# Three edits to a two-block transformer kernel: where Down's operand lies, a mixer with blocks of 8, and products without a result

## The chip, the cores and the metric

The kernel runs on one core of one Trainium2 chip. The metric is the device time of one execution in microseconds; three runs were timed. One more execution was recorded by the hardware profiler, and every row below comes from that one. TensorE is called PE, VectorE DVE, ScalarE ACT, GpSimd POOL. A product is one matrix instruction of PE.

## The reference

256 rows of width 1024 pass through two layers of a first model and one layer of a second. In short:

```python
for i in range(2):
    x = x + 0.5 * swiglu(rms_norm(x, g[0]), gate, up, down)      # D_FF = 2816
    x = x + (even_mixer if i == 0 else mla_mixer)(rms_norm(x, g[1]))
    x = x + 0.5 * swiglu(rms_norm(x, g[2]), gate, up, down)
    x = x + per_layer_embedding(rms_norm(x, g[3]), p[i], ...)    # rms_norm(sigmoid(h Wg) * (p Wp))
x = x + hybrid_mixer(rms_norm(x, ...))
x = x + swiglu(rms_norm(x, ...), gate_up, down)
return rms_norm(x, norm_final)
```

So there are five feed-forward blocks. The even mixer, the "first mixer", splits `h @ w_in` into six parts; four of them (q, f, i, g) go to a gated linear recurrence with 4 heads of 128 and chunks of 64:

```python
b = cumsum(log f)                                    # inside a chunk of 64
scores[t, s] = sum_d q[t, d] * k[s, d] * exp(b[t, d] - b[s, d])    for s <= t
o = scores @ v + (q * exp(b)) @ state                # state carries over the chunks
o = rms_norm(o, out_norm) * silu(g)                  # norm over each head's 128
mixed = concat([a_out, o]) @ w_out
```

## The kernel before, in words

**Layout.** The residual stream `x` lies feature-major: eight tiles of 128 features by 256 rows. Each normalized operand is split in two float32r tiles, `hh` (high part) and `hl` (the rest); each weight likewise in `whi` and `wlo`. One product of the reference is three on PE: hh·whi, hl·whi, hh·wlo, each over 128 x 128 weights and 256 columns. Weights come in pieces of 2,048 columns by DMA on SP's queue; ACT copies each half to `whi` (L259) and DVE subtracts for `wlo` (L260). Six buffers of each exist, so the copy of half n+6 waits until PE has used half n.

**Places.** Tiles are laid out in a partition in the order in which they are first asked for, pool by pool. `hh` and `hl` (16 tiles of 1,024 bytes) begin at byte 99,776 and all lie at 448 modulo 512. The work tiles `big` (13 buffers of 4,096 bytes) begin at byte 153,664 and lie at 64 modulo 512. A feed-forward block first runs gate and up (1,056 products, moving operand `hh` or `hl`), then Down (528 products: 8 outputs, 22 inner blocks, 3 each), whose moving operand is the split activation `aT`, kept in `big` tiles. PE passes from the last product of gate and up to the first of Down without anything between. Weights lie at 128 modulo 512 throughout. A tile `pad` of 48 columns, which nothing uses, lies between `gu` and `nz`; what comes after it moves with its size: `nz`, `sqa`, `ny`, `rb`, `sg`, `pr`, `big` among them.

**Statistics.** `Stat.begin` multiplies the squares by a column of ones (moving operand `ones`, weights `sqa` or `sq`), DVE makes `ny`, the inverse root, and `Stat.finish` spreads it over the partitions with two transposes (`ident`, `ny`). In a feed-forward block these two groups stand among the first 160 products of gate and up; behind the second of them about 910 products run to the end of gate and up with no other group between.

**First mixer.** The scores inside a chunk of 64 are summed from a base (blocks of 4, one reference point for each block) and four levels (4, 8, 16, 32). Each level costs DVE two subtractions, two multiplications of 128x512 and two `COPY_PREDICATED` (L669), ACT one Exp, and PE eight full float32 products of 128 columns, which the trace records as sixteen. Then come the gates `g`, feature-major (`fm`, 96 products), the spatial part (`gm`), the attention output `og`, 16 ones-records for its norm, the first 72 products of the output projection, 8 broadcasts of the inverse root, DVE's multiplication (L821), the split (L273, L274), and the other 120 products.

**Order.** A scheduler writes each engine's instructions in one fixed order; an engine runs them in that order and waits at a semaphore where an operand isn't there yet.

Of the kernel before, what the change touches and what calls it, by code (L numbers as in the profile page):

```python
# [10 lines left out]
FT = mybir.dt.float32  # L11
FR = mybir.dt.float32r
# [5 lines left out]
P = 128  # L18
# [41 lines left out]
class Stat:  # L60
# [8 lines left out]
    def begin(self, ins=None, quick=False):  # L69
        k, nc = self.k, self.k.nc  # L70
        ps = k.aux()
        with k.behind(ins):
            last = len(self.parts) - 1
            for n, t in enumerate(self.parts):
                for b in range(NB):
                    k.mm(ps[:, b : b + 1], t[:, b * P : (b + 1) * P], k.ones, n == b == 0, n == last)
        v = k.tiny(NB, "nv")
        with k.tc.high_priority():
            y = None
            if quick:  # L80
                y = k.tiny(NB, "ny", bufs=6)
                self.mark = nc.scalar.activation(y, ps[:, :NB], AF.Sqrt, scale=1.0 / self.n, bias=k.eps).ins
            nc.vector.tensor_scalar(v, ps[:, :NB], 1.0 / self.n, EPS, op0=OP.mult, op1=OP.add)
            if quick:
                nc.vector.reciprocal(y, y)
        self.r = k.rsqrt(v, NB, y)

    def finish(self, ins=None, copy=True):
        k = self.k
        self.pb = pb = k.aux()[:, :T]  # L90
        with k.behind(ins):
            for b in range(NB):
                k.bcast(pb[:, b * P : (b + 1) * P], self.r[:, b : b + 1].to_broadcast([P, P]))
        return self.copy() if copy else self

    def copy(self):
# [10 lines left out]
class Kern:  # L107
# [54 lines left out]
    def mm(self, out, l, r, start=True, stop=True):  # L162
        return self.nc.tensor.matmul(out, l, r, start=start, stop=stop, skip_group_check=True).ins  # L163

    def behind(self, ins):
        return self.tc.issue_after(ins) if ins is not None else nullcontext()


    def constants(self):
# [40 lines left out]
            for c in range(D)  # L210
        ]

        self.sp.tile([P, 48], FT, name="pad", bufs=1)
        self.eps = cp.tile([P, 1], FT, name="eps")
        nc.vector.memset(self.eps, EPS)
        nc.scalar.activation(self.tiny(1, "nz"), self.ones, AF.Silu)
# [82 lines left out]

    def bcast(self, out, col, w=P):  # L300

        self.nc.tensor.transpose(out, col, self.ident)  # L302


    def sq_add(self, src, j, own=False):
# [196 lines left out]
    def ple(self, i, proj, rstd, post, gain, fill=None):  # L502
# [14 lines left out]

        self.fm([(("ple_w_gate", i), (d * P, P)) for d in range(D)], self.hT, evac, [2, 2, 2, 1, 1], k_first=True, stat=rstd)
        self.late = (self.piece + 2, 1), self.mark
        post_r = self.sq_end().now()  # L520
        more = fill() if fill else None


# [54 lines left out]
    def even(self, rstd, prep):  # L578
# [75 lines left out]
        def scores(kx, qx, lvl):  # L654
            for b in range(NB):
                ps = self.aux()
                for h in range(H):
                    o = slice(h * T + b * P, h * T + (b + 1) * P)
                    self.mm(ps[:, h * P : (h + 1) * P], kx[:, o], qx[:, o])
                p3 = ps.rearrange("p (h t) -> p h t", h=H)  # L660
                if lvl > 3:

                    l = 32 * (lvl - 3)
# [9 lines left out]


        d = self.big()
        b4 = bb.rearrange("p (m l) -> p m l", l=4)
        nc.vector.tensor_tensor(
            d.rearrange("p (m l) -> p m l", l=4), b4, b4[:, :, 1:2].to_broadcast([P, 256, 4]), op=OP.subtract
        )
        eq, ek = self.big(), self.big()  # L680
        nc.scalar.activation(eq, d, AF.Exp)
# [13 lines left out]
            nc.vector.tensor_tensor(xh[:, :, 1, :], xh[:, :, 1, :], qh[:, :, 1, :], op=OP.mult)  # L695
            scores(x, x, n + 1)

        level(0, 4)
        vi = self.cut([512, 512])

        def evac_i(b, ps):
# [1 line left out]

        self.tm(src, (2048, 512), self.hT, evac_i)

        for n, l in ((1, 8), (2, 16), (3, 32)):
            level(n, l)


# [8 lines left out]
        scores(x, x, 5)  # L718


        y = self.big()
# [19 lines left out]
        nc.scalar.activation(scA4[:, :, P:], ps.rearrange("p (h t) -> p h t", h=H), AF.Copy)  # L741


        sg = self.big()

        def evac_g(c, ps):
            o = slice(c * T, (c + 2) * T)
            self.scaled(sg[:, o], ps, rstd.rb)
            nc.scalar.activation(sg[:, o], sg[:, o], AF.Silu)

        self.fm([(src, (2560 + h * P, P)) for h in range(4)], self.hT, evac_g)

        gm = []
# [28 lines left out]
                gm.append((c, hi, lo))  # L784


        og = self.big()
        hs = self.aux()
        sqs = []
        for j in range(2):  # L790
            ps = self.aux()
            for u in range(2):
                h = 2 * j + u
                o = slice(u * T, (u + 1) * T)
                self.mm(ps[:, o], vi[0][:, h * P : (h + 1) * P], scA[:, h * T : (h + 1) * T], True, False)
                self.mm(
                    ps[:, u * T + P : (u + 1) * T], vi[1][:, h * P : (h + 1) * P],
                    scB[:, h * P : (h + 1) * P], False, True,
                )
# [4 lines left out]
            o = slice(j * 512, (j + 1) * 512)  # L804
            nc.vector.tensor_tensor(og[:, o], ps, sg[:, o], op=OP.mult)
# [5 lines left out]
        hv = self.tiny(8, "nv")  # L811
        nc.vector.tensor_scalar(hv, hs[:, :8], 1.0 / P, EPS, op0=OP.mult, op1=OP.add)
        hr = self.rsqrt(hv, 8)
        ks = []
        for j in range(2):
# [4 lines left out]
            o = slice(j * 512, (j + 1) * 512)  # L820
            nc.vector.tensor_tensor(og[:, o], og[:, o], ps, op=OP.mult)  # L821
            g2 = self.big(FR)
            hi, lo = g2[:, :512], g2[:, 512:]
            self.split(hi, lo, og[:, o], self.col("hgrn_out"))
            for u in range(2):
                ks.append((4 + 2 * j + u, hi[:, u * T : (u + 1) * T], lo[:, u * T : (u + 1) * T]))
# [590 lines left out]
    def load_small(self):  # L1417
        nc, a, cp = self.nc, self.a, self.cp

        def const(name, cols, dt=FT, eng=None):  # L1420
            t = cp.tile([P, cols], dt, name="k_" + name)
            (eng or nc.gpsimd).dma_start(t, a[name])
            return t

        self.tri = const("tri", P)
        self.amask = const("amask", 384)
        self.lvl = const("lvl", 4 * P, I32)
# [108 lines left out]
def constants():  # L1536
# [115 lines left out]
```

## Time and profile before

| what | value |
|---|---|
| median of 3 runs | 1332.64 us (1331.53 to 1332.75) |
| the profiled execution's own time | 1331.74 us |
| its span | 1330.0 us |
| PE busy | 1305.2 us (98%) |
| DVE, ACT, POOL busy | 922.9, 726.4, 76.1 us |
| mean granted clock of PE | 0.995 |

The span is what the profiler saw, the execution's own time has the start and end around it, 1.74 us. The profiled execution was 0.90 us faster than the median. PE is busy nearly all the time, so the table of busy shares alone says little: what counts is how fast PE's products follow each other in each stage, and the few places where it stands.

### The profile page before, as it was taken

How to read it: one execution, taken by the hardware profiler on the slowest of the kernel's cores; microseconds unless marked ns; L12 is line 12 of the kernel's file. 1: busy time of each engine (PE TensorE's matmuls, PEld its weight loads, DVE VectorE, ACT ScalarE, POOL GpSimd, SP SyncE). 2: the span in 40 equal slices, each digit the busy share in tenths (PEclk: the TensorE clock that was granted, in tenths of full speed). 3: DMA queues.
4: the chain of work that ended last, by engine and by line, in shares of the span. 5: the costliest groups of instructions: out<-in, count | busy, mean ns of one | idle time of the engine just before them, and what ended most of it. 6: DMA issues, size and time to landing. Idle time of an engine off the chain costs nothing.

```text
span 1330.0 us, 25894 instructions
## 1 busy us (share of the span) xinstructions
PE 1305.2 (98%) x10830; PEld 1275.3 (96%) x10830; DVE 922.9 (69%) x1528; ACT 726.4 (55%) x1110; POOL 76.1 (6%) x94
## 2 busy tenths in 40 slices
PE   9999999999999999999999899999998999999997
PEld 8999999899999999999999679999998998999997
DVE  7866657978666657966556867777557897867643
ACT  6555546646555456655545566554445685655542
POOL 3000010002000001000000002000002000200001
PEclk9999999999999999999999999999999999999999
DMA  8755555245555554465546313655555344455541
GB/s 320 262 190 187 174 196 181 95 162 188 190 190 188 185 210 159 163 219 190 190 162 220 127 64 116 205 191 196 185 186 183 135 142 143 164 207 198 194 159 64
DMA packets 34933, 235.50 MB, mean 177 GB/s; under 512 B 4016, under 2 KB 4784, under 8 KB 7168
## 3 DMA queue, kind: packets, MB, share of 16 engines
q1 hardware_dynamic: 32976, 229.98, 50.0%
q0 software_dynamic: 832, 2.47, 0.6%
q8 instruction: 85, 1.39, 0.4%
q10 hardware_dynamic: 1008, 1.40, 0.3%
q14 instruction: 32, 0.26, 0.1%
HBM read 232.78 MB, written 1.05 MB: 176 GB/s over the span
## 4 chain that ended last, share of the span: by engine, by line
PE 74%; DVE 5%; ACT 2%; issue 1%; DVEq 0%; ACTq 0%
PE acc L163 69%; PE aux L163 4%; DVE wlo L260 1%; PE aux L302 0%; ACT whi L259 0%; PE aux L1130 0%; DVE big L1175 0%; DVE qs L961 0%; ACT hh L273 0%; ACT at L1132 0%; DVE kv L961 0%; ACT ae L1122 0%; ACT big L949 0%; DVE big L514 0%; DVE big L429 0%
## 5 line engine op out<-in xcount | busy, mean ns | idle before, releaser
L260 DVE TENSOR_TENSOR wlo<-wraw,whi 128x1024 fp32r<-128x1024 f32 (+1 forms) x440 | 531.7, 1222 | 253.1 <-ACT whi L259 164.2
L259 ACT ACTIVATE whi<-wraw 128x1024 fp32r<-128x1024 f32 (+1 forms) x440 | 451.3, 1047 | 308.4 <-PE acc L163 221.4
L163 PE MATMUL acc<-hh,whi 128*128 128x256 f32 x2192 | 328.3, 279 | 3.4 <-ACT hh L538 3.1
L163 PE MATMUL acc<-hl,whi 128*128 128x256 f32 x2192 | 327.3, 278 | 0.2 <-DVE hl L543 0.2
L163 PE MATMUL acc<-hh,wlo 128*128 128x256 f32 x2192 | 326.3, 278 | 1.1 <-DVE wlo L260 1.1
L163 PEld LDWEIGHTS acc<-hh,whi 128*128 128x128 f32 x2192 | 286.0, 188 | 5.4 <-ACT hh L538 3.8
L163 PEld LDWEIGHTS acc<-hh,wlo 128*128 128x128 f32 x2192 | 286.0, 188 | 1.6 <-DVE wlo L260 1.4
L163 PEld LDWEIGHTS acc<-hl,whi 128*128 128x128 f32 x2192 | 286.1, 188 | 0.4 <-DVE hl L543 0.4
L163 PE MATMUL acc<-big,whi 128*128 128x256 f32 x2032 | 271.7, 280 | 0.0
L163 PEld LDWEIGHTS acc<-big,whi 128*128 128x128 f32 x2032 | 256.4, 189 | 0.4 <-ACT big L270 0.2
L163 PE MATMUL acc<-big,wlo 128*128 128x256 f32 x1016 | 161.7, 280 | 0.0
L163 PEld LDWEIGHTS acc<-big,wlo 128*128 128x128 f32 x1016 | 137.6, 189 | 0.0
L318 POOL TENSOR_TENSOR sqa<-sqa,sq 128x256 f32<-128x256 f32 x72 | 65.0, 903 | 1119.2 <-ACT sq L317 1117.1
L429 DVE TENSOR_TENSOR gu<-acc,rb 128x512 f32<-128x512 f32 (+1 forms) x122 | 81.9, 678 | 50.4 <-PE acc L163 50.1
L273 ACT ACTIVATE hh<-x,cols 128x256 fp32r<-128x256 f32 x64 | 30.3, 503 | 82.7 <-DVE x L468 79.2
L270 ACT ACTIVATE big<-pr 128x256 fp32r<-128x256 f32 x114 | 45.9, 409 | 52.0 <-DVE pr L447 50.2
L445 ACT ACTIVATE sg<-gu 128x256 f32<-128x256 f32 x110 | 44.8, 411 | 38.7 <-DVE gu L429 38.5
L271 DVE TENSOR_TENSOR big<-pr,big 128x256 fp32r<-128x256 f32 x114 | 47.8, 426 | 21.0 <-ACT big L270 21.0
L447 DVE TENSOR_TENSOR pr<-sg,gu 128x256 f32<-128x256 f32 x110 | 45.4, 419 | 2.2 <-ACT sg L445 2.2
L274 DVE SCALAR_TENSOR_TENSOR hl<-x,cols,hh 128x256 fp32r<-128x256 f32 x64 | 38.0, 619 | 8.6 <-ACT hh L273 8.3
L163 PE MATMUL aux<-big 128*128 128x128 f32 (+5 forms) x260 | 37.6, 310 | 0.8 <-DVE big L683 0.8
L317 ACT ACTIVATE sq<-x 128x256 f32<-128x256 f32 x62 | 23.9, 405 | 24.3 <-DVE x L470 18.2
(297 smaller groups left out, 788.5 us busy)
## 6 DMA issues: line engine op xcount, KB each, us to landing
wraw<-wts SPq DMA_DIRECT2D x216, 1024.0 KB, 4.9
wraw<-wts SPq DMA_DIRECT2D x4, 256.0 KB, 4.9
wraw<-wts SPq DMA_DIRECT2D x2, 512.0 KB, 5.4
x<-xT SPq DMA_DIRECT2D x2, 256.0 KB, 5.2
big<-wsT POOLq DMA_DIRECT2D x1, 512.0 KB, 13.3
gu<-pT ACTq DMA_DIRECT2D x2, 256.0 KB, 3.1
out<-big SPq DMA_DIRECT2D x2, 256.0 KB, 2.3
out<-big ACTq DMA_DIRECT2D x2, 256.0 KB, 2.5
```

Source lines behind the costliest of these rows:

```text
L163: return self.nc.tensor.matmul(out, l, r, start=start, stop=stop, skip_group_check=True).ins
L259: nc.scalar.activation(hi[:, i], s, AF.Copy)
L260: nc.vector.tensor_tensor(lo[:, i], s, hi[:, i].bitcast(FT), op=OP.subtract)
L270: a = nc.scalar.activation(hi, src, AF.Copy)
L271: b = nc.vector.tensor_tensor(lo, src, hi.bitcast(FT), op=OP.subtract)
L273: a = nc.scalar.activation(hi, src, AF.Copy, scale=scale)
L274: b = nc.vector.scalar_tensor_tensor(lo, src, scale, hi.bitcast(FT), op0=OP.mult, op1=OP.subtract)
L317: nc.scalar.activation(q, src, AF.Square)
L318: self.mark = nc.gpsimd.tensor_tensor(self.sq[0], self.sq[0], q, op=OP.add).ins
L429: self.nc.vector.tensor_tensor(out.rearrange("p (u t) -> p u t", u=n), ps.rearrange("p (u t) -> p u t", u=n), rb.unsqueeze(1).to_broadcast ...
L445: self.mark = nc.scalar.activation(sg, gu[:, :T], AF.Silu).ins
L447: nc.vector.tensor_tensor(pr, sg, gu[:, T:], op=OP.mult)
```

## The change

Three things. The tile `pad` shrinks from 48 to 16 columns and the constant `lvl` by 512 bytes, so `big` begins at byte 153,024, at 448 modulo 512, as `hh` and `hl` do; every other tile behind `pad` moves by the same 128 bytes modulo 512. The first mixer's base takes blocks of 8 and loses a level; its gates are made token-major (`tm`, 48 products of 512 columns), and so is the output with its norm: a reduction on DVE in place of the ones, a multiplication, and 8 transposes in place of the broadcasts. Behind the second embedding's last product, 8, 5 and 5 full float32 products of `ident` and `tri` into a bank that nobody reads are placed ahead of the sum, ahead of the spreading and after it.

```diff
+    def keep_on(self, ins, n):
+        ps = self.aux()
+        with self.tc.high_priority(), self.behind(ins):
+            for _ in range(n):
+                m = self.mm(ps[:, :P], self.ident, self.tri)
+        return m
...
-        self.sp.tile([P, 48], FT, name="pad", bufs=1)
+        self.sp.tile([P, 16], FT, name="pad", bufs=1)
...
-        post_r = self.sq_end().now()
+        post_r = self.sq_end()
+        if fill:
+            post_r.now()
+        else:
+            post_r.begin(self.keep_on(self.last, 8), quick=True)
+            post_r.finish(self.keep_on(post_r.summed, 5), copy=False)
+            self.keep_on(post_r.spread, 5)
...
-        b4 = bb.rearrange("p (m l) -> p m l", l=4)
+        b8 = bb.rearrange("p (m l) -> p m l", l=8)
...
-        level(0, 4)
...
-        for n, l in ((1, 8), (2, 16), (3, 32)):
+        for n, l in ((0, 8), (1, 16), (2, 32)):
             level(n, l)
...
-        self.fm([(src, (2560 + h * P, P)) for h in range(4)], self.hT, evac_g)
+        sg = self.cut([512, 512])
+        def evac_g(b, ps):
+            nc.scalar.activation(sg[b], ps, AF.Silu, scale=rstd.r[:, b : b + 1])
+        self.tm(src, (2560, 512), self.hT, evac_g)
...
+        for b in range(NB):
             ps = self.aux()
+            for h in range(H):
+                o = slice(h * P, (h + 1) * P)
+                self.mm(ps[:, o], scA4[:, h, b * P : (b + 1) * P], vi[0][:, o], h == 0, b == 0)
+                if b:
+                    self.mm(ps[:, o], scB3[:, h, :], vi[1][:, o], False, True)
             q = self.tmp(512, "gu", bufs=3)
             nc.scalar.activation(q, ps, AF.Square)
-            for n in range(4):
-                self.mm(hs[:, j * 4 + n : j * 4 + n + 1], q[:, n * P : (n + 1) * P], self.ones)
...
+            nc.vector.tensor_reduce(hs[:, b * H : (b + 1) * H], by_head(q), axis=AX.X, op=OP.add)
+            nc.vector.tensor_tensor(og[b], ps, sg[b], op=OP.mult)
...
+            nc.vector.tensor_tensor(
+                by_head(og[b]), by_head(og[b]), hr[:, b * H : (b + 1) * H].unsqueeze(2).to_broadcast([P, H, P]), op=OP.mult
+            )
             ps = self.aux()
             with self.behind(self.last):
-                for n in range(4):
-                    self.bcast(ps[:, n * P : (n + 1) * P], hr[:, j * 4 + n : j * 4 + n + 1].to_broadcast([P, P]))
...
+                for h in range(H):
+                    nc.tensor.transpose(ps[:, h * P : (h + 1) * P], og[b][:, h * P : (h + 1) * P], self.ident)
+            self.split(hi4[:, :, b, :], lo4[:, :, b, :], by_head(ps), self.col("hgrn_out"))
...
-    lvl = [(s // 4 == t // 4) & (s <= t)]
-    for n in (4, 8, 16):
+    lvl = [(s // 8 == t // 8) & (s <= t)]
+    for n in (8, 16):
```

Outside the first mixer and the end of the second embedding, no instruction changes its place on PE, DVE or ACT. Three places of the order follow.

DVE, from the norm of the mixer's output (`nv` or `hs` is the mean of squares, `nb`, `ny`, `nz` the steps of its inverse root, `wlo` a weight half) to the multiplication by it. Before:

```order
L812 TENSOR_SCALAR nv<-aux 128x8
L291 TENSOR_SCALAR nb<-nv 128x8
L292 TENSOR_SCALAR ny<-nb 128x8
...
L296 SCALAR_TENSOR_TENSOR nz<-nz,nv 128x8
L260 TENSOR_TENSOR wlo<-wraw,whi 128x1024
L297 SCALAR_TENSOR_TENSOR ny<-nz,ny 128x8
...
L297 SCALAR_TENSOR_TENSOR ny<-nz,ny 128x8
L260 TENSOR_TENSOR wlo<-wraw,whi 128x1024
L821 TENSOR_TENSOR big<-big,aux 128x512 x2
```

And now:

```order
L820 TENSOR_SCALAR hs<-hs 128x8
L268 TENSOR_TENSOR wlo<-wraw,whi 128x1024
L299 TENSOR_SCALAR nb<-hs 128x8
L268 TENSOR_TENSOR wlo<-wraw,whi 128x1024
L300 TENSOR_SCALAR ny<-nb 128x8
L268 TENSOR_TENSOR wlo<-wraw,whi 128x1024
L303 TENSOR_TENSOR nz<-ny 128x8
...
L305 SCALAR_TENSOR_TENSOR ny<-nz,ny 128x8
L825 TENSOR_TENSOR big<-big,ny 128x512 x2
L268 TENSOR_TENSOR wlo<-wraw,whi 128x1024
L282 SCALAR_TENSOR_TENSOR big<-aux,cols,big 128x4x128 x2
```

Three weight halves now stand inside the chain of the inverse root, where one stood, with nine short steps behind the third.

PE, in the output projection (`acc<-big`): the 8 broadcasts stood behind its 72nd product; the 8 transposes, of the normalized output, now stand behind the 86th and the 87th. Before and now:

```order
L163 MATMUL acc<-big,wlo 128x256
L302 MATMUL aux<-ident,ny 128x128 x8
L163 MATMUL acc<-big,whi 128x256 x2
```

```order
L163 MATMUL acc<-big,whi 128x256 x2
L831 MATMUL aux<-ident,big 128x128 x4
L163 MATMUL acc<-big,wlo 128x256
L831 MATMUL aux<-ident,big 128x128 x4
L163 MATMUL acc<-big,whi 128x256 x2
```

The wait moved with them: the broadcasts needed `ny` alone, the transposes need the multiplied output.

PE, from the end of the second embedding's gate to the first product of the hybrid mixer (`sqa` and `sq` are squares, `k_tri,ident` the added products), now:

```order
L163 MATMUL acc<-hh_119,wlo 128x256
L163 MATMUL aux<-k_tri,ident 128x128 x8
L163 MATMUL aux<-ones,sqa 128x1 x2
L163 MATMUL aux<-ones,sq 128x1 x4
L163 MATMUL aux<-k_tri,ident 128x128 x5
L310 MATMUL aux<-ident,ny 128x128 x2
L163 MATMUL aux<-k_tri,ident 128x128 x5
L163 MATMUL acc<-hh_105,whi 128x256 x3
```

The eighteen `k_tri,ident` rows are new; the others stand as before.

## Rows read from the trace of the kernel before

**Rows 1.** The page, part 1: busy time, share of the span, instructions.
```profile
PE 1305.2 (98%) x10830; PEld 1275.3 (96%) x10830; DVE 922.9 (69%) x1528; ACT 726.4 (55%) x1110; POOL 76.1 (6%) x94
```

**Rows 2.** PE by stretch: start:end, length, busy (instructions that reach in), granted clock, DMA.
```profile
30.00:130.00 100.00, 100.00 (x852) 1.00 0.62 213
135.00:195.00 60.00, 60.00 (x512) 1.00 0.51 176
330.00:430.00 100.00, 100.00 (x852) 1.00 0.55 183
435.00:495.00 60.00, 60.00 (x532) 1.00 0.54 187
...
836.00:936.00 100.00, 100.00 (x885) 1.00 0.58 192
940.00:1000.00 60.00, 60.00 (x512) 1.00 0.51 176
```

**Rows 3.** What PE waited for from 195 to 307 us: us, times, longest.
```profile
PE aux L163 <- DVE big L683: 0.8, 1, 0.8
```

**Rows 4.** Timeline of PE in the first mixer: start, us, instruction, count.
```profile
256.56 3.73 PE L163 MATMUL aux<-big 128*128 128x128 f32 x32
...
280.42 1.05 PE L163 MATMUL aux<-ones,gu 128*128 128x1 f32 x8
281.33 1.55 PE L163 MATMUL aux<-big 128*128 128x256 f32 x8
...
291.88 1.03 PE L302 MATMUL aux<-ident,ny 128*128 128x128 f32 x8
```

**Rows 5.** Timelines of DVE and ACT at the end of the first mixer.
```profile
287.40 1.22 DVE L260 TENSOR_TENSOR wlo<-wraw,whi 128x1024 fp32r<-128x1024 f32 x1 [1.01 <-ACT whi L259]
...
288.94 0.17 DVE L296 SCALAR_TENSOR_TENSOR nz<-nz,nv 128x8 f32<-128x8 f32 x1
289.14 0.17 DVE L297 SCALAR_TENSOR_TENSOR ny<-nz,ny 128x8 f32<-128x8 f32 x1
...
292.51 1.28 DVE L821 TENSOR_TENSOR big<-big,aux 128x512 f32<-128x512 f32 x2 [1.06 <-PE aux L302]
...
294.85 1.41 DVE L274 SCALAR_TENSOR_TENSOR big<-big,cols 128x512 fp32r<-128x512 f32 x2
...
289.13 1.06 ACT L259 ACTIVATE whi<-wraw 128x1024 fp32r<-128x1024 f32 x1 [1.77 <-PE acc L163]
```

**Rows 6.** Timeline of all engines at the end of the second embedding.
```profile
1022.10 1.07 PE L163 MATMUL acc<-hh,wlo 128*128 128x256 f32 x8
...
1024.02 0.61 PE L163 MATMUL aux<-ones,sqa 128*128 128x1 f32 x4 [0.86 <-POOL sqa L318]
...
1026.08 0.61 PE L163 MATMUL aux<-ones,sq 128*128 128x1 f32 x4 [1.00 <-DVE sq L314]
...
1027.94 0.69 PE L302 MATMUL aux<-ident,ny 128*128 128x128 f32 x2 [1.26 <-DVE ny L297]
...
1030.21 1.01 PE L163 MATMUL acc<-hh,whi 128*128 128x256 f32 x3 [1.57 <-ACT hh L538]
1030.38 0.48 DVE L543 SCALAR_TENSOR_TENSOR hl<-x,cols,hh 128x256 fp32r<-128x256 f32 x1
...
1031.63 0.48 DVE L543 SCALAR_TENSOR_TENSOR hl<-x,cols,hh 128x256 fp32r<-128x256 f32 x1
...
1033.64 0.32 PE L163 MATMUL acc<-hh,wlo 128*128 128x256 f32 x1
```

**Rows 7.** All engines by stretch: PE, PEld, DVE, ACT, POOL busy, then granted clock.
```profile
1027.00:1033.00 6.00, 3.48 (x14) 3.08 (x15) 4.97 (x17) 2.45 (x7) 0.00 (x0) 0.50 0.53 178
1034.00:1044.00 10.00, 10.00 (x87) 10.00 (x86) 8.82 (x16) 7.18 (x12) 0.00 (x0) 1.00 0.00 0
...
740.00:762.00 22.00, 17.59 (x88) 13.60 (x89) 21.16 (x47) 12.06 (x18) 0.00 (x0) 1.00 0.33 102
```

More of the change, by code (lines that the diff above doesn't have):

```diff
@@ L75, in begin @@
                 for b in range(NB):
-                    k.mm(ps[:, b : b + 1], t[:, b * P : (b + 1) * P], k.ones, n == b == 0, n == last)
+                    self.summed = k.mm(ps[:, b : b + 1], t[:, b * P : (b + 1) * P], k.ones, n == b == 0, n == last)
         v = k.tiny(NB, "nv")
@@ L92, in finish @@
             for b in range(NB):
-                k.bcast(pb[:, b * P : (b + 1) * P], self.r[:, b : b + 1].to_broadcast([P, P]))
+                self.spread = k.bcast(pb[:, b * P : (b + 1) * P], self.r[:, b : b + 1].to_broadcast([P, P]))
         return self.copy() if copy else self
@@ L300, in bcast @@
     def bcast(self, out, col, w=P):
-        self.nc.tensor.transpose(out, col, self.ident)
+        return self.nc.tensor.transpose(out, col, self.ident).ins
     def sq_add(self, src, j, own=False):
@@ L660, in scores @@
                 p3 = ps.rearrange("p (h t) -> p h t", h=H)
-                if lvl > 3:
-                    l = 32 * (lvl - 3)
+                if lvl > 2:
+                    l = 32 * (lvl - 2)
                     for o in range(0, P, 2 * l):
@@ L675, in even @@
         d = self.big()
-        b4 = bb.rearrange("p (m l) -> p m l", l=4)
+        b8 = bb.rearrange("p (m l) -> p m l", l=8)
         nc.vector.tensor_tensor(
-            d.rearrange("p (m l) -> p m l", l=4), b4, b4[:, :, 1:2].to_broadcast([P, 256, 4]), op=OP.subtract
+            d.rearrange("p (m l) -> p m l", l=8), b8, b8[:, :, 3:4].to_broadcast([P, 128, 8]), op=OP.subtract
         )
@@ L717, in even @@
         nc.vector.tensor_tensor(xh[:, :, 1, :], xh[:, :, 1, :], qh[:, :, 1, :], op=OP.mult)
-        scores(x, x, 5)
+        scores(x, x, 4)
         y = self.big()
@@ L741, in even @@
         nc.scalar.activation(scA4[:, :, P:], ps.rearrange("p (h t) -> p h t", h=H), AF.Copy)
[L744 to L749, printed above, removed]
-        self.fm([(src, (2560 + h * P, P)) for h in range(4)], self.hT, evac_g)
+        sg = self.cut([512, 512])
+        def evac_g(b, ps):
+            nc.scalar.activation(sg[b], ps, AF.Silu, scale=rstd.r[:, b : b + 1])
+        self.tm(src, (2560, 512), self.hT, evac_g)
         gm = []
@@ L784, in even, with by_head @@
                 gm.append((c, hi, lo))
[L787 to L790, printed above, removed]
-            ps = self.aux()
[L792 to L799, printed above, removed]
+        og = self.cut([512, 512])
+        hs = self.tiny(8, "hs")
+        def by_head(t):
+            return t.rearrange("p (h d) -> p h d", h=H)
+        for b in range(NB):
+            ps = self.aux()
+            for h in range(H):
[3 more added lines that the diff above has]
+                    self.mm(ps[:, o], scB3[:, h, :], vi[1][:, o], False, True)
             q = self.tmp(512, "gu", bufs=3)
             nc.scalar.activation(q, ps, AF.Square)
-            for n in range(4):
-                self.mm(hs[:, j * 4 + n : j * 4 + n + 1], q[:, n * P : (n + 1) * P], self.ones)
-            o = slice(j * 512, (j + 1) * 512)
-            nc.vector.tensor_tensor(og[:, o], ps, sg[:, o], op=OP.mult)
+            nc.vector.tensor_reduce(hs[:, b * H : (b + 1) * H], by_head(q), axis=AX.X, op=OP.add)
+            nc.vector.tensor_tensor(og[b], ps, sg[b], op=OP.mult)
         banks = [self.acc() for _ in range(4)]
@@ L809, in even @@
         self.out_proj(wo, gm[:3], banks, True, False)
[L811 to L815, printed above, removed]
+        nc.vector.tensor_scalar(hs, hs, 1.0 / P, EPS, op0=OP.mult, op1=OP.add)
+        hr = self.rsqrt(hs, 8)
+        hi, lo = self.big(FR), self.big(FR)
+        hi4, lo4 = (t.rearrange("p (h b t) -> p h b t", h=H, b=NB) for t in (hi, lo))
+        for b in range(NB):
+            nc.vector.tensor_tensor(
+                by_head(og[b]), by_head(og[b]), hr[:, b * H : (b + 1) * H].unsqueeze(2).to_broadcast([P, H, P]), op=OP.mult
+            )
             ps = self.aux()
             with self.behind(self.last):
-                for n in range(4):
-                    self.bcast(ps[:, n * P : (n + 1) * P], hr[:, j * 4 + n : j * 4 + n + 1].to_broadcast([P, P]))
[L820 to L826, printed above, removed]
+                for h in range(H):
+                    nc.tensor.transpose(ps[:, h * P : (h + 1) * P], og[b][:, h * P : (h + 1) * P], self.ident)
+            self.split(hi4[:, :, b, :], lo4[:, :, b, :], by_head(ps), self.col("hgrn_out"))
+        ks = [(4 + h, hi[:, h * T : (h + 1) * T], lo[:, h * T : (h + 1) * T]) for h in range(H)]
         self.out_proj(wo, gm[3:], banks, False, False)
@@ L1426, in load_small @@
         self.amask = const("amask", 384)
-        self.lvl = const("lvl", 4 * P, I32)
+        self.lvl = const("lvl", 3 * P, I32)
         self.scanm = const("scanm", 512)
```

## The prediction

> **What bounds the kernel now.** I read the page's busy times first. PE is busy 98% of the span [rows 1], so a microsecond is worth something only if it is PE's: fewer products, faster products, or one of the few places where PE stands. Then PE by stretch, to see how fast its products follow each other. In a stretch without a gap, length by count gives the spacing (a little low, since an instruction that only reaches in is counted). The reader is to see that there are two speeds at one granted clock of 1.00. Gate and up of the first two feed-forward blocks: 100 us by 852, 117.4 ns. Gate and up of the fourth: 100 by 885, 113.0 ns. Down of the second block: 60 by 532, 112.8 ns; Down of the first and the fourth: 60 by 512, 117.2 ns [rows 2]. Blocks three and five read as the fourth, so there are six such rows of fast gate and up followed by slow Down. All of a stretch runs at one speed, and in four blocks of five the speed changes at the step from gate and up to Down, where nothing waits and nothing changes but the operand: moving tiles at 448 modulo 512 give way to tiles at 64. The first block is slow on both sides. So the speed is something that PE carries along; the step of 128 bytes disturbs it, and can do so in both directions (slow to fast in block two, fast to slow in three, four and five). The rows don't say what it is.
>
> Last I read the first mixer and the end of the second embedding. In the mixer's 112 us PE waits only 0.8 us, for the base's operand [rows 3]: it is PE-bound. At the end of the second embedding it stands 0.86, 1.00, 1.26 and 1.57 us [rows 6], and the clock is at its lower level, 0.50, from 1027 to 1033 [rows 7].
>
> **Part one, the place.** With `big` at 448 the step disappears: Down's operand lies as gate and up's. I take it that the speed is then kept through the step. The difference is 4.4 ns a product (117.4 - 113.0). Down has 528 products: 2.3 us. Blocks three, four and five stay fast: -6.9 us. Block two stays slow through Down and the 48 products of the embedding's projection behind it, which read `big` too and run as Down does: 576 x 4.4 = +2.5. Block one stays as it is. Behind blocks three and four the first 48 products of the next stage follow at an unchanged place and may stay fast, 0.2 us each; I take half of the 0.4. Sum: -4.6 us. The bounds are nothing (the place doesn't matter) and, should every Down be fast, -7.3.
>
> Here the Trainium skill speaks against the edit. The page "TensorE: Matmul & The Clock Gate", section "Wait — 56ns, not 53.3ns?", gives the spacing of warm products as columns by 2.4 GHz and a fixed 2.5 ns, 109.2 ns for 256 columns by that estimate, with no word of addresses; "SBUF — State Buffer", section "SBUF: two separate sides", says that PE waits for nobody at its ports. By these the part gives 0 and the sum is 4.6 us smaller. The trace agrees with neither spacing: it has two, 113 and 117 ns [rows 2].
>
> **Part two, the first mixer.** PE's work first. A level is half of the 32 records that take 3.73 us: -1.8. The ones for the norm cost 0.91 us from their start to the next group's (280.42 to 281.33), twice: -1.8. The norm's products were two groups of 8 records, recorded 1.55 us long with their overlap, and are now 24 records of some 0.11, 2.7: about equal. 8 transposes stand for 8 broadcasts of 1.03 [rows 4]; the gates are 48 products of 512 columns for 96 of 256. Together -3.6 us. DVE loses a level too, so it isn't later than before at the scores, where it was just in time.
>
> Then the new wait. The third weight half inside the chain of the inverse root needs a buffer that PE frees after 48 products of the output projection (a half holds eight weight blocks, 24 products). From the projection's first product: 48 x 0.1175 = 5.6; ACT's copy 1.06, DVE's subtraction 1.22: 7.9; nine short steps, one every 0.20 us (288.94 to 289.14): 9.7; the first of the two multiplications, 0.64: 10.4 [rows 5]. PE is at the transposes after 86 products, 10.1. It waits 0.3, and behind it all the rest of the projection. The second multiplication ends at 11.0, another weight half takes DVE to 12.2, the two splits (1.41 for both) to 13.6 [rows 5]; PE, with 0.3 of waiting and 1.0 of transposes, asks for the last of them after about 100 products, at 13.1: 0.5 more. Before, the broadcasts needed `ny` of 289.3 at 291.88 [rows 4, 5], so they had 2.5 us to spare; that margin is spent. Part two: -3.6 + 0.8 = -2.8, bounds -3.6 (no wait) and 0 (see the rivals).
>
> **Part three, the added products.** By the records of 0.11 us (3.73 for 32 [rows 4]), two for a float32 product of 128 columns, 8 of them take 1.8 us: from 1023.0, where the gate's records end (1022.10 and eight of 0.117), to 1024.8. The two groups of ones behind them, at most 0.61 each by their record, end at 1026.0; the last square was there only at 1026.08 [rows 6]. Nothing is late. Five take 1.1, from 1026.7 to 1027.8, and `ny` came for 1027.94; five more end at 1029.3, and `hh` came for 1030.21. Of 4.7 us of standing some 1.5 are left. In the second mixer PE stood 4.4 of 22 us and the clock held at 1.00 [rows 7], so I take it that it holds here. What that saves: before, 16 products ran from 1030.21 to 1033.8 at the lower level (0.50, that is 1.2 GHz). At the higher, three run, the fourth waits for `hl` of the first block (1030.38 + 0.48 = 1030.86), nine are through at 1032.0, the second block's `hl` comes at 1031.63 + 0.48 = 1032.11 [rows 6], and the sixteenth is through at 1032.5: -1.3 us. Behind that PE runs without a gap [rows 7], so it is kept. Bounds: 0, if the clock falls all the same, and -1.7, if no `hl` were waited for (16 slots of 0.22 less 16 of 0.117).
>
> **Sum.** -4.6 - 2.8 - 1.3 = -8.7 us. The profiled execution's own time was 1331.74: 1323.0. It lay 0.9 below the median of the runs, so the median comes to 1323.9.
>
> **The rivals.**
>
> *The second block turns fast.* What sets the speed of its 912 products behind the statistics' second group is what happens at that group. What PE did ahead of that group is the end of the first mixer, which the change rewrites, and `sqa` and `ny` lie 128 bytes on; either could change it. For it: in three blocks of five this stretch is fast. Against it: the order at that place is unchanged. Gate and up gain 912 x 4.4 = 4.0 and Down doesn't lose 2.5: 1323.9 - 6.5 = 1317.4.
>
> *The place doesn't matter*, and every Down stays as it is, or the speed is settled anew at each stage. For it: Down of block two is fast at 64, and gate and up of blocks one and two are slow at 448, so no place has a speed of its own. Against it: the change of speed at exactly the step. Without part one: 1323.9 + 4.6 = 1328.5. The Trainium skill's rule of a fixed spacing ("TensorE: Matmul & The Clock Gate") is this rival.
>
> *Slower: a fast gate and up turns slow.* The weights of the statistics' products are `sqa` and `ny`, and they move by 128 bytes as well. If that turns the stretch behind them slow, a block loses 4.0 in gate and up and, its Down now keeping that speed, the 2.3 counted as gained: +6.3. One block gives 1330.2, two 1336.5, all three 1342.8; from two blocks on the change is a loss. For it: such groups stand wherever the speed of a gate and up was settled. Against it: their timing is unchanged.
>
> *The mixer's new wait is longer.* If the third weight half waits for the next release, 24 products later, the chain is 2.8 us later and part two gives nothing: 1326.7. The order puts it near: PE has 0.3 us less than it needs.
>
> **How the numbers follow.** Chances: forecast 0.50 (its own range 1322 to 1326, with the clock's 1.3 and the lead's 0.2), second block fast 0.15, place without effect 0.20, fast stretches lost 0.08 (half of it one block), longer wait 0.07. The range must hold the first, the second, the third and the last; with the third's own spread it is 1317.0 to 1329.0. About 0.2% of the time, 2.7 us, is what a measurement of this kernel can tell from no change. Faster than 1330.0: all but the slow case, less some of the third should two parts fail together: 0.88. Within 0.2%: 0.08. Slower: 0.04.
>
> **What would show it.** PE by stretch: Down of blocks three to five at 113 ns, of block two at 117; gate and up as before in all five. In the mixer, 16 records fewer on `lvl`'s products, none on `ones,gu`, and a wait of 0.3 to 1 us at the transposes for DVE. At the second embedding's end, granted clock 1.00 from 1027 on, and the ones at the same distance behind the gate. I am wrong if a gate and up has another speed than before, if Down's speed differs from that of the gate and up ahead of it, or if PE waits more than 1.5 us in the projection.

## The result, and the profile after

The changed kernel takes 1322.47 us in the median of 4 runs (1316.75 to 1322.95), the kernel before 1332.7 (1331.53 to 1334.59, 4 runs): a ratio of 0.9917, 95% interval 0.9891 to 0.9942. The forecast was 1323.9 in a range of 1317.0 to 1329.0. The profiled execution took 1322.39, 9.35 less than that of before (1331.74). One of the four runs lies 5.7 us below the median; the other three are within 0.6 us of each other. The experiments come back to it; there, the ratio of place_448_next leaves out two slow runs (1337.2 and 1340.39 us), its median does not.

The first lines of the page of the changed kernel, the span and the busy times, which answer to [rows 1]:

```profile
span 1320.7 us, 25813 instructions
...
PE 1299.7 (98%) x10794; PEld 1267.6 (96%) x10794; DVE 918.9 (70%) x1522; ACT 725.2 (55%) x1109; POOL 75.6 (6%) x94
```

PE is still busy 98% of the span; 5.5 of the 9.3 us are busy time of PE, the rest is idle time. PE by stretch, in the stretches of [rows 2], reads:

```profile
30.00:130.00 100.00, 100.00 (x851) 1.00 0.62 213
135.00:195.00 60.00, 60.00 (x512) 1.00 0.50 176
330.00:430.00 100.00, 100.00 (x851) 1.00 0.57 194
435.00:495.00 60.00, 60.00 (x512) 1.00 0.51 178
...
836.00:936.00 100.00, 100.00 (x885) 1.00 0.56 191
940.00:1000.00 60.00, 60.00 (x532) 1.00 0.54 193
```

Gate and up stand as before (851 slow, 885 fast). Down has changed sides: that of the second block from 532 to 512, that of the fourth from 512 to 532. In all five blocks Down now has the speed of its gate and up (for blocks 3 and 5 by the starts below).

Where the 9.3 us came from is read from the starts of the stages' first products on PE:

| stage begins | before | after | gained up to here |
|---|---|---|---|
| first mixer | 206.86 | 206.69 | 0.17 |
| block 2 | 306.94 | 303.32 | 3.62 |
| Down of block 2 | 432.24 | 428.62 | 3.62 |
| first embedding's gate | 497.52 | 496.46 | 1.06 |
| Down of block 3 | 651.35 | 650.33 | 1.02 |
| second mixer | 713.53 | 710.17 | 3.36 |
| Down of block 4 | 937.96 | 934.49 | 3.47 |
| second embedding's gate | 1000.14 | 994.33 | 5.81 |
| last mixer, first wide product | 1055.48 | 1048.17 | 7.31 |
| Down of block 5 | 1257.63 | 1250.37 | 7.26 |
| last product | 1323.00 | 1313.50 | 9.50 |

The mixer gives 3.45, Down of block 2 takes 2.56 back, Down of blocks 3, 4 and 5 gives 2.34, 2.34 and 2.24, the second embedding 1.50. All else together is within 0.2 us. The 48 products that open the second mixer and the second embedding read their operand at an unchanged place; they too ran fast now (5.80 us in place of 6.02), but later waits took much of these 0.22 us back: 0.11 is left of the first when Down of block 4 begins.

**The first mixer.** PE's work and its waits, by the same view over the whole mixer, for the kernel before:

```profile
206.86:306.94 100.08, 99.28 (x755) 1.00 0.42 147
```

and for the changed kernel, with what PE waited for there (us, times, longest):

```profile
206.69:303.32 96.63, 95.33 (x684) 1.00 0.43 152
...
PE aux L163 <- DVE big L698: 0.8, 1, 0.8
PE aux L831 <- DVE big L825: 0.3, 1, 0.3
PE acc L163 <- DVE big L282: 0.2, 1, 0.2
```

The work falls by 3.95 us, and two waits come in, 0.33 and 0.20, the two that were foreseen: the transposes wait for DVE's multiplication, and a product of the projection waits for a split. The timelines of PE and DVE there show them:

```profile
274.06 4.89 PE L163 MATMUL aux<-big 128*64 128x128 f32 x56
...
289.41 0.63 PE L831 MATMUL aux<-ident,big 128*128 128x128 f32 x4 [0.33 <-DVE big L825]
...
290.01 0.63 PE L831 MATMUL aux<-ident,big 128*128 128x128 f32 x4
...
292.38 0.39 PE L163 MATMUL acc<-big,whi 128*128 128x256 f32 x1 [0.20 <-DVE big L282]
...
285.62 1.23 DVE L268 TENSOR_TENSOR wlo<-wraw,whi 128x1024 fp32r<-128x1024 f32 x1
...
288.57 1.29 DVE L825 TENSOR_TENSOR big<-big,ny 128x512 f32<-128x512 f32 x2
289.78 1.22 DVE L268 TENSOR_TENSOR wlo<-wraw,whi 128x1024 fp32r<-128x1024 f32 x1
290.92 1.40 DVE L282 SCALAR_TENSOR_TENSOR big<-aux,cols,big 128x512 fp32r<-128x512 f32 x2
```

The third weight half stands at 285.62 in the chain of the inverse root, and the multiplication begins 2.9 us later. The norm's 16 records on `ones,gu` [rows 4] are gone from the view.

**The second embedding's end.** The timeline of PE, which answers to the PE lines of [rows 6]:

```profile
1016.98 1.95 PE L163 MATMUL aux<-k_tri,ident 128*128 128x128 f32 x16
1018.76 0.50 PE L163 MATMUL aux<-ones,sqa 128*128 128x1 f32 x4
...
1020.05 0.61 PE L163 MATMUL aux<-ones,sq 128*128 128x1 f32 x4 [0.34 <-DVE sq L322]
1020.52 1.36 PE L163 MATMUL aux<-k_tri,ident 128*128 128x128 f32 x10
1022.01 0.40 PE L310 MATMUL aux<-ident,ny 128*128 128x128 f32 x2
1022.25 1.28 PE L163 MATMUL aux<-k_tri,ident 128*128 128x128 f32 x10
1023.99 0.62 PE L163 MATMUL acc<-hh,whi 128*128 128x256 f32 x3 [0.46 <-ACT hh L553]
```

Four idle times of 0.86 to 1.57 us have become two that the view names, 0.34 and 0.46. The granted clock over 25 us around this place (last three figures: clock, DMA share, GB/s) is at its higher level throughout:

```profile
1010.00:1035.00 25.00, 23.99 (x203) 1.00 0.29 105
```

In the kernel before, the same stretch reads 0.86.

### The profile page after: what moved, and what is told of

The parts are those of the page before. It is cut to its first block, busy times and chain, and to the rows that moved or that the text cites. A ratio compares the mean times of both kernels' runs of the same rounds, so it can differ in the third digit from the quotient of the medians.

```text
span 1320.7 us, 25813 instructions
## 1 busy us (share of the span) xinstructions
PE 1299.7 (98%) x10794; PEld 1267.6 (96%) x10794; DVE 918.9 (70%) x1522; ACT 725.2 (55%) x1109; POOL 75.6 (6%) x94
## 4 chain that ended last, share of the span: by engine, by line
PE 73%; DVE 4%; ACT 2%; issue 1%; DVEq 0%; ACTq 0%
PE acc L163 69%; PE aux L163 4%; DVE wlo L268 1%; ACT whi L267 1%; PE aux L310 0%; PE aux L1137 0%; DVE big L1182 0%; DVE qs L968 0%; ACT at L1139 0%; DVE kv L968 0%; ACT ae L1129 0%; ACT big L956 0%; ACT big L1186 0%; DVE big L522 0%; DVE x L548 0%
## 5 line engine op out<-in xcount | busy, mean ns | idle before, releaser
L163 PE MATMUL acc<-hh,whi 128*128 128x256 f32 x2160 | 323.1, 279 | 2.2 <-ACT hh L553 2.0
L163 PE MATMUL acc<-hh,wlo 128*128 128x256 f32 x2160 | 321.5, 278 | 0.7 <-DVE wlo L268 0.7
L163 PE MATMUL acc<-hl,whi 128*128 128x256 f32 x2160 | 321.8, 278 | 0.3 <-DVE hl L558 0.2
L163 PEld LDWEIGHTS acc<-hh,whi 128*128 128x128 f32 x2160 | 281.3, 188 | 3.5 <-ACT hh L553 2.5
L163 PEld LDWEIGHTS acc<-hh,wlo 128*128 128x128 f32 x2160 | 281.2, 188 | 1.5 <-DVE wlo L268 1.3
L163 PEld LDWEIGHTS acc<-hl,whi 128*128 128x128 f32 x2160 | 281.4, 188 | 0.7 <-DVE hl L558 0.7
L163 PE MATMUL acc<-big,whi 128*128 128x256 f32 x2032 | 268.8, 278 | 0.2 <-DVE big L282 0.2
L163 PEld LDWEIGHTS acc<-big,whi 128*128 128x128 f32 x2032 | 253.5, 188 | 0.6 <-DVE big L282 0.4
```

## Experiments

All times are device microseconds. Measured again beside the experiments, in four groups of runs, the kernel before had medians of 1334.0 (31 runs), 1333.8 (24), 1335.6 (7) and 1331.9 (7), and spread from 1327 to 1339, far more than in the three runs shown ahead of the prediction. Each kernel's ratio is to the kernel before in its own group.

**The place of `big`, four values.** Is it the step of the operand that matters, and which steps?

```diff
             if f % 2 == 0:
+                if f == 0 and not hasattr(self, "a2"):
+                    self.sp.tile([P, 32], FT, name="step", bufs=1)   # 64, 96, 128 in the others
                 self.a2 = self.big(FR)
```

> The changed kernel with an unused tile of 128 bytes ahead of `big`: `big` is back at 64 modulo 512, while `sqa`, `ny` and the other small tiles stay where the change put them. Theory (PE carries its speed, and the step of the moving tiles' place disturbs it): Down of blocks 3, 4 and 5 at 117.8 ns again and that of block 2 at 113.3, gate and up as in the changed kernel; 3 x 2.35 - 576 x 4.4 ns = +4.5 us, 1327 us. Rival one (the small tiles' places did it): Down stays as in the changed kernel, 1322.4. Rival two (the speed is settled anew at each stage): Downs mixed, without regard to the gate and up ahead of them.

> As before, with 256 bytes: `big` at 192 modulo 512, another step than 448 or 64. Theory: there is a step again, so Down of blocks 3 to 5 does not keep the fast speed (+7.0), and a slow gate and up (blocks 1 and 2) may turn fast in Down (-2.3 to -2.5 each): 1324.5 to 1329.5. If only the step of exactly 128 bytes disturbs: 1322.4. Rival one: 1322.4.

> As before, with 384 bytes: `big` at 320 modulo 512. Theory: as for 192, 1324.5 to 1329.5, and should block 1 or 2 turn fast at one of the three places and not at the others, the speed is a matter of how far the place steps and not of a step as such. Rival one: 1322.4.

> With 512 bytes ahead of `big` (a small tile of the last mixer with one buffer in place of two, to have room): every `big` tile is 512 bytes on, at 448 modulo 512 as in the changed kernel, and at another place modulo 1024. Theory (modulo 512 counts): no Down changes its speed against its gate and up, 1322.4, or some 6.5 less if a slow block turns fast. Rival (any move disturbs, or the place modulo 1024 counts): like place_64, 1327.

Times: place_64 1331.82 (ratio 0.9974, interval 0.9954 to 0.9995), place_192 1329.54 (0.9962, 0.9936 to 0.9988), place_320 1330.21 (0.9975, 0.9952 to 0.9998), place_448_next 1329.49 (0.9937, 0.9906 to 0.9968). By the medians the last one would be 0.9966 (1329.49 by 1333.98); its two longest runs may be executions with few fast blocks (below). The medians miss most of the expected numbers; in the profiles, gate and up is not fast in the same blocks each time, and in place_64 and place_320 the second mixer was 1.5 us longer, with a dip of the clock (end of this section). The speeds by stretch decide. For place_64, Down of blocks 2, 3 and 4, by PE's stretches as above (50 us: 443 is fast, 427 slow):

```profile
440.00:490.00 50.00, 50.00 (x443) 1.00 0.52 180
...
650.00:700.00 50.00, 50.00 (x427) 1.00 0.53 187
...
940.00:990.00 50.00, 50.00 (x427) 1.00 0.51 180
```

It is the pattern of [rows 2] once more: slow to fast in block 2, fast to slow in 3 and 4. Only `big` and what lies behind it moved, `sqa` and `ny` did not, so the small tiles' places are not the cause. For place_192, gate and up of block 3 (80 us: 708 is fast, 681 slow), then Down of blocks 3, 4 and 5:

```profile
560.00:640.00 80.00, 80.00 (x708) 1.00 0.60 203
655.00:705.00 50.00, 50.00 (x443) 1.00 0.53 188
850.00:930.00 80.00, 80.00 (x682) 1.00 0.54 185
945.00:995.00 50.00, 50.00 (x427) 1.00 0.49 174
...
1262.00:1312.00 50.00, 50.00 (x444) 1.00 0.40 143
```

Down keeps its speed at 192, although 192 is not 448. And gate and up of block 4 (682) is slow in this execution. For place_320, gate and up of block 3, then Down of blocks 3, 4 and 5:

```profile
560.00:640.00 80.00, 80.00 (x708) 1.00 0.60 200
655.00:705.00 50.00, 50.00 (x427) 1.00 0.54 189
...
945.00:995.00 50.00, 50.00 (x427) 1.00 0.50 180
...
1262.00:1312.00 50.00, 50.00 (x427) 1.00 0.41 146
```

All three lose the fast speed. In place_448_next every Down has its gate and up's speed, with every `big` tile 512 bytes on. Counted over the ten profiles in which the rows lie at 448 (five blocks each; that of before and four told of below among them, draws not):

| step from the rows to `big`, modulo 512 | fast stays fast | fast turns slow | slow turns fast | slow stays slow |
|---|---|---|---|---|
| 0 (448) | 16 | 0 | 0 | 14 |
| 256 (192) | 2 | 0 | 0 | 3 |
| 128 (64) | 0 | 5 | 2 | 3 |
| 384 (320) | 0 | 3 | 0 | 2 |

So, from rows at 448, what counts is whether the step is a multiple of 256; the expectation for 192 was wrong. The rows lay at 448 in all ten, so the step isn't told apart from `big`'s own place: steps of 128 and 384 both put it at 64 modulo 256. Against its own place alone stands Down of block 2, fast at 64 in the kernel before and in place_64.

**The changed kernel in more executions.** No edit.

> The changed kernel once more, in more executions. The profiles so far show gate and up of blocks 3, 4 and 5 fast in 11 of 15 cases and those of blocks 1 and 2 slow in all. Theory (each execution draws the speed of a gate and up anew at the statistics, and in the changed kernel Down follows it): the times lie on a ladder of 6.4 us (1440 products of 4.44 ns), 1322.4 with three fast blocks, 1328.8 with two, 1335.2 with one, 1316 with four, and the kernel before, where a fast block is worth only 4.05, or 2.5 by Down alone, spreads less. Rival (the speed belongs to the kernel): 1322.4 throughout, the spread of the times coming from elsewhere.

1325.04 in the median of 9 runs, ratio 0.993, interval 0.9901 to 0.9959. The nine times: 1315.87, 1316.21; 1322.81, 1323.61, 1325.04; 1329.11, 1329.69, 1329.74, 1330.99. The three groups fit the ladder of 6.4 us: four, three and two fast blocks. Profiles back two of its steps: three fast blocks in the profiled run here (1323.61) and in that of 1322.39, two in place_448_next at 1328.41. Four stand in no profile, and the two profiles of this kernel have the same blocks fast; that the speed of a gate and up is settled anew in each execution is concluded from the times. The run of 1316.75 in the first measurement has its place on the ladder. (The expectation counts 11 fast of 15; the profiles have 12.)

**The place alone.** Kernel before, and only:

```diff
-        self.sp.tile([P, 48], FT, name="pad", bufs=1)
+        self.sp.tile([P, 16], FT, name="pad", bufs=1)
```

> The kernel before with only the unused tile shortened, so that `big` is at 448; mixer and embedding as before. Theory (steps of the prediction add up): Down of each block at the speed of its gate and up, 2.35 us less for each of blocks 3 to 5 that is fast and 2.5 more for block 2: 1328 with three fast blocks. Mixer 3.5 and second embedding 1.5 us longer than in the changed kernel. Rival (the place does nothing by itself): as the kernel before in the same job, 1332 to 1334.

1328.89 (12 runs, 1323.15 to 1335.72), ratio 0.997, interval 0.995 to 0.9989: 4 us. The profiled execution (1335.72) is the kernel's slowest. Gate and up and Down of its block 1, then gate and up of block 3 and Down of it:

```profile
30.00:120.00 90.00, 90.00 (x797) 1.00 0.66 229
135.00:185.00 50.00, 50.00 (x443) 1.00 0.53 184
...
560.00:640.00 80.00, 80.00 (x681) 1.00 0.58 197
655.00:705.00 50.00, 50.00 (x427) 1.00 0.53 185
```

Here block 1 is fast (797 in 90 us; at the slow speed, 117.5 ns, it would be 766) and blocks 3 and 4 are slow: no block has a speed of its own in all these kernels. Its mixer takes 100.11 us, as before (100.08), so the mixer's gain is not the place's.

**Without the added products.**

```diff
-        if fill:
-            post_r.now()
-        else:
-            post_r.begin(self.keep_on(self.last, 8), quick=True)
-            post_r.finish(self.keep_on(post_r.summed, 5), copy=False)
-            self.keep_on(post_r.spread, 5)
+        post_r.now()
```

> The changed kernel without the 18 added products behind the second embedding. Theory: the clock falls to 0.50 for some 6 us again and the stretch from that embedding's start to the last mixer's start is 1.5 us longer: 1324 with three fast blocks. Rival (the clock holds without them, as its fall was chance): within 0.3 us of the changed kernel in that stretch.

1326.11 (10 runs, 1321.39 to 1334.55), ratio 0.9958, interval 0.9934 to 0.9981. The times do not separate it from the changed kernel, the stretch does: from the second embedding's gate to the last mixer's wide products 56.19 us, against 53.84 in both profiles of the changed kernel: 2.35 longer, where 1.5 was expected. In the kernel before it is 55.34. The clock in this stretch, no_added:

```profile
1010.00:1035.00 25.00, 20.36 (x146) 0.80 0.29 104
```

From 1020 to 1028 it stood at 0.50, longer than in the kernel before [rows 7]. Without the products the clock fell here in all three profiles that lack them (this one, the kernel before, place_alone); with them it fell in one of eleven (finish_52, next), and for a shorter time.

**A later second group of the statistics.**

```diff
-        self.lead, self.when = 2, (0, 48)
+        self.lead, self.when = 2, (0, 52)
...
-when=(48, 96) if lead == 1 else self.when
+when=(48, 100 if gate[0] == ("ffn_w_gate", 0, 1) else 96) if lead == 1 else self.when
```

> The changed kernel with the second group of the statistics four products later in block 2 (two in block 1). In block 2 PE waited 0.09 us there for `ny`, and the gap was 345 to 355 ns against 253 in blocks 3 to 5. Theory (a group without a wait lets the speed turn fast, as in blocks 3 to 5): gap 253 and gate and up fast in block 2, Down with it, 6.6 us: 1316. Rival (the wait has nothing to do with it, as in block 1, which is slow at a gap of 250): slow, 1322.

1323.21 (6 runs), ratio 0.993, interval 0.9909 to 0.9952. The gap in block 2 falls from 355 to 250 ns, and gate and up stays slow: 851 instructions in 330 to 430, as in the changed kernel. The wait for `ny` is not why block 2 is slow. A side result: with the added products in place the clock still dipped here, and the stretch took 54.36 us:

```profile
1010.00:1035.00 25.00, 24.53 (x199) 0.93 0.32 116
```

**Groups as draws.**

```diff
                     reached(m)
+                    if len(chunks) > 20 and count % 96 == 0 and stat is not None and stat.rb is not None:
+                        self.draw(stat, m, count // 96 % 2)
...
+    def draw(self, stat, ins, kind):
+        ps = self.aux()
+        with self.behind(ins):
+            if kind:
+                for b in range(NB):
+                    self.bcast(ps[:, b * P : (b + 1) * P], stat.r[:, b : b + 1].to_broadcast([P, P]))
+            else:
+                self.mm(ps[:, :P], self.ident, self.ident)
```

> The changed kernel with small groups of products without a result in every gate and up, one behind each 96 products, in turn two transposes of `ident` with `ny` (the products of the statistics' second group) and one product of `ident` with `ident`: 10 groups in a block, 0.1 to 0.25 us each, some 8 us in all; 50 changes or non-changes of the speed to be read from one profile. Theory (the speed is settled at an interruption): it changes only at such groups, in both directions. If a group turns slow fast in most cases and leaves fast alone, one or two of them in blocks 1 and 2 would pay (6.4 us each, less 0.2). Rival (small groups alone don't change it, the waits on the statistics do): every gate and up runs at one speed to its end.

1355.02 (2 runs), ratio 1.0156, interval 1.0114 to 1.0199. In block 3 the statistics' second group left PE fast, and the first added group, 36 products later, turned it slow. PE's timeline there, eight products to a row: 0.90 us from row to row ahead of the group, 0.94 behind it:

```profile
555.62 1.07 PE L163 MATMUL acc<-hl,whi 128*128 128x256 f32 x8
556.52 1.07 PE L163 MATMUL acc<-hh,wlo 128*128 128x256 f32 x8
557.43 0.38 PE L319 MATMUL aux<-ident,ny 128*128 128x128 f32 x2
...
558.59 1.10 PE L163 MATMUL acc<-hl,whi 128*128 128x256 f32 x8
559.53 1.10 PE L163 MATMUL acc<-hh,wlo 128*128 128x256 f32 x8
```

Behind every other added group, in all five blocks, PE is slow. So a group can take the fast speed away (seen once), no added group gave it, and the idea that a group is a fair draw is wrong. In blocks 2, 4 and 5 the first added group stands right behind the statistics' second group, with no product between, so whether the statistics alone would have left PE fast there isn't shown. The time fits if blocks 3, 4 and 5 would have been fast: three fast blocks lost (19.2), and 50 groups of some 0.22 us (11.0), on 1322.4 make 1352.6.

**The rows at other remainders of 128.**

```diff
+        cp.tile([P, 16], FT, name="off")   # 64 bytes; 8 and 24 columns in the others
         self.hT = [
```

> The changed kernel with 64 unused bytes ahead of the rows' tiles: `hh` and `hl`, `big` and all small tiles are 64 bytes on, the rows at 0 modulo 512; the weights stay at 128. Theory (the two speeds come from how the moving tiles' place stands to that of the weights in steps of 128 bytes): with another remainder modulo 128 the speeds or how often each is drawn differ, so not 113.3 and 117.8 or not fast in 3 of 5 gate and ups. Rival (only the distance of two moving tiles from each other counts): the same two speeds, Down as its gate and up, times on the same ladder, 1316 to 1335.

> The changed kernel with 32 unused bytes ahead of the rows' tiles: rows at 480 modulo 512, 96 modulo 128 (the weights at 128, 0 modulo 128). At 64 modulo 128 the spacing was 113.3 or 117.8 in steady stretches, at 0 modulo 128 118.7 to 119 in a mean over records of 115 to 123, and 29 us more in all. Theory (the place of the rows modulo 128 against that of the weights sets the spacings): other spacings again, steady or not; if every stretch takes 113 ns, 1309 us, if every stretch takes 119 ns, 1353. Rival (only 0 modulo 128 is special, any other place is as 64): 113.3 and 117.8, on the ladder from 1316 to 1335.

> As before with 96 bytes: rows at 32 modulo 512 and modulo 128. Theory: as for off_32, another spacing, and not the same one unless the two sides of 64 are alike. Rival: 113.3 and 117.8, on the ladder from 1316 to 1335.

off_64 1353.79 (4 runs; ratio 1.015, interval 1.0117 to 1.0183), off_32 1364.58 (4; 1.0242, 1.0216 to 1.0268), off_96 1345.5 (4; 1.011, 1.0067 to 1.0153). PE from 30 to 130 us in gate and up of block 1 for off_64:

```profile
30.00:130.00 100.00, 100.00 (x845) 1.00 0.62 212
```

for off_32:

```profile
30.00:130.00 100.00, 100.00 (x835) 1.00 0.62 211
```

and for off_96:

```profile
30.00:130.00 100.00, 100.00 (x855) 1.00 0.62 213
```

That is 118.3, 119.8 and 117.0 ns a product by count (117.5 and 113.0 in the changed kernel's slow and fast stretches above), at the same granted clock, and the records within a stretch run through several spacings (115 to 123 in off_64) instead of one. Of the four remainders only 64, that of both kernels here, has stretches at 113 ns. Off_96 has two speeds as well; gate and up of block 3, then of block 5:

```profile
560.00:640.00 80.00, 80.00 (x684) 1.00 0.58 198
...
1175.00:1255.00 80.00, 80.00 (x676) 1.00 0.54 185
```

The first is 117.0 ns by count, as in blocks 1, 2 and 4, the second 118.3, and Down follows it in all five blocks. The expectations' rival, that only one remainder is special, is wrong; none of the three beats the changed kernel.

**The clock elsewhere.** The traces of all runs show a second thing that differs from execution to execution. In six of 14 profiles the clock fell for a short time behind the first embedding, as in changed_again,

```profile
527.00:534.00 7.00, 5.52 (x31) 0.76 0.35 139
```

and in four in the second mixer (place_64, place_320, off_64, off_96). Each dip costs some 1.5 us: from the first embedding's gate to the sums of block 3's statistics changed_again took 46.64 us, the first profile of the same kernel 45.10; the second mixer took 104.67 in place_64, and 103.12 in the kernel before, where the clock held. So two executions with the same fast blocks can differ by 1.5 or 3 us.

## Why the prediction was right, step by step

**Two speeds that PE carries, and a step that disturbs them: right.** The step was put too narrowly: a step of 256 bytes keeps the speed as well. The forecast that block 2 loses 2.5 us and blocks 3, 4 and 5 gain 2.3 each came in at 2.56, and 2.34, 2.34 and 2.24. The 48 products behind blocks 3 and 4 were both fast, but of their 0.22 us each little was kept: 0.11 behind block 3 (second mixer 103.01 us after 103.12, though five other profiles with these 48 fast and the clock up took 103.18 to 103.21), and 0.07 behind block 4 (53.84 us to the last mixer, against 53.91 in place_64, where these 48 are slow). That it comes to the forecast's half of 0.4 is luck. The term: -4.6 forecast, -4.5 measured. Its bound of -7.3, "should every Down be fast", forgets the slow Down of block 1, another 2.3.

**The Trainium skill's fixed spacing** ("TensorE: Matmul & The Clock Gate", section "Wait — 56ns, not 53.3ns?") was the rival in which the place does nothing. The ladder and the three off kernels decide against it: by count 256 columns took 113.0, 117.0, 117.5, 118.3 or 119.8 ns, by the operand's place and by what PE did before.

**The first mixer: the mechanism right, two terms a little off.** The work fell by 3.95, not 3.6. From start to start, the level gave 1.8 and the ones 1.8, as forecast. The rest lies in two terms that were put at nothing. What the prediction calls the norm's products takes 2.70 us (4.65 from 274.06 to the projection's start at 278.71 for 56 records, less 1.95 for the 32 narrower ones, as before), just as forecast, but the two groups of before took 2.92 and not the same. The gates take 11.60 for 11.78. The eight transposes (0.38 and 0.39) cost as much as the broadcasts did, whose record of 1.03 [rows 4] is 0.79 to the next product's start. The waits were 0.33 and 0.20, where 0.3 and 0.5 were forecast. Sum -3.45 for -2.8. The rival of a longer wait did not happen: the third weight half came at 285.62, between two steps of the chain, as the sum had it.

**The added products: right, from a premise that doesn't hold in general.** The stage gave 1.50 for 1.3: 0.4 up to the first product behind the statistics, of which 0.2 comes from the 48 fast products at its start, and 1.1 behind it, where the clock had been low. Place_64, with the products and with those 48 as slow as in the kernel before, took 1.43 less there than that kernel; no_added took 2.35 more than the changed kernel. So what the products are worth depends on how long the clock would have stayed low. The premise was that PE may stand 4.4 of 22 us with the clock at 1.00, as in the second mixer [rows 7]. But in four of 14 profiles the clock fell in just that mixer, and with the products it still dipped once (finish_52, 0.5 us). So the clock holds in that mixer more often than not, and not surely.

**What the prediction took for granted and should not have.** It read "gate and up of blocks 3, 4 and 5 is fast" from one profile as a trait of the kernel. The times say that it is drawn anew in each execution; over ten profiles, of nine kernels, blocks 3 to 5 were fast in 25 of 30 cases, blocks 1 and 2 in 1 of 20. Three runs of before within 1.2 us gave no hint. There a fast gate and up gained 4.05 us (912 products of 4.44 ns) and Down nothing, and a slow one in some cases got 2.3 to 2.5 back in Down; now a fast block is worth 6.4. So the change does two things: it lowers the mean while most draws are fast, and it stretches the spread. The rivals held the sizes (6.5 for a block turned fast, 6.3 for one turned slow), but as single events, with the kernel's other executions left out; and the range's upper end is passed by four of the nine runs of changed_again. That three of the first four runs lay where three blocks are fast, and the median so close to the forecast, is in part luck. Had most draws been slow, the place would have been a loss of 2.5 us in block 2 with nothing against it. By these counts the place is worth 2.35 x 2.5 fast blocks of three less 2.5, about 3.4 us, where 4.6 was forecast; place_alone measured 4 (0.3%, interval 0.1 to 0.5%).

## What to carry to other kernels

A stage without a gap is timed by count over length, and a second speed there is worth looking for in several profiles, since one profile shows one draw. Two operands that PE reads one behind the other belong, in a kernel like this, at places that differ by a multiple of 256 bytes (tried from one place of the first alone), if the first is fast more often than not. A product without a result is cheap where it fills a wait that would let the clock fall, and can cost PE its higher speed where it stands inside an unbroken stretch.

## What was not expected of the hardware

The spacing of 256-column products at a granted clock of 1.00 depends on the moving tile's place modulo 128 (the weights at 0 of it), by count: 117.0 or 118.3 ns at 32, 113.0 or 117.5 at 64, 119.8 at 96 and 118.3 at 0. At 64 each of the two is steady for 900 products. What settles the one or the other at the statistics is open. It is not the wait ahead of the second group: gaps of 250 ns (finish_52, block 2) and of 253 (place_alone, blocks 3 and 4) both stand ahead of slow stretches, and 253 stands ahead of most stretches at 113 ns too. And it is nothing that the program fixes, if the ladder is read rightly, since one program's times fall on three of its steps.
